# Layer 0's input norm scaled on VectorE alone, and silu's product moved ahead in its place

## The chip, the cores and the metric

The kernel runs on one core of a Trainium2 chip. The core has five engines with a queue each: TensorE (PE in the profile, its weight loads PEld), VectorE (DVE), ScalarE (ACT), GpSimd (POOL) and SyncE (SP), which here issues the DMAs. Each engine takes its instructions strictly in the order in which they were queued; engines wait for one another by semaphores. The metric is the time on the device in microseconds (us), the median of several runs; less is better.

## The reference

One inference step of two layers, a gated DeltaNet layer (layer 0) and an RWKV-7 layer (layer 1), over 1024 prompt tokens with 16 learned tokens ahead of them, and over 8 samples of 8 tokens: 1104 rows of width 1024. Both parts of the change lie in layer 0, whose start is

```python
def rmsnorm(x, w):
    xf = x.astype(jnp.float32)
    return xf * lax.rsqrt(jnp.mean(xf * xf, -1, keepdims=True) + RMS_EPS) * w.astype(jnp.float32)
...
def causal_conv(u, buf, w):
    ...
    for j in range(1, CONV_W):
        y = y + up[:, j:j + T] * w[:, j]
    return jax.nn.silu(y), up[:, up.shape[1] - (CONV_W - 1):]
...
    proj = xn @ w_in
    ...
    qkv, new_buf = causal_conv(qkv, conv_buf, conv_w)
```

The normed input `xn` is multiplied by the input projection; q, k and v go through a convolution over four tokens and silu; then come L2 norms of q and k, the chunked delta rule per head with a triangular solve, a gated norm and the output projection. There are 8 q/k heads and 16 value heads.

## The kernel before, in words

**The front.** The 1104 rows are cut into 9 blocks, numbered 0 to 8, of 128 rows (block 8 has 80). For each block `input_load` issues the DMA, `input_squares` takes the sum of squares of each row on ACT, `input_rates` makes the rate of each row (the mean on DVE, a power on POOL at line 160, and three small DVE operations at lines 162 to 164, one step of Newton's method), `input_scale` multiplies the block by the rate and by the norm's weight `nwb`, and `input_turn` transposes it on PE into PSUM (eight transposes), copies it as the high half into SBUF on ACT (line 361) and takes the low half as a difference on DVE (line 365). High and low halves serve a product in three passes, which stands in for full float32.

There are two ways of scaling in the kernel before. Blocks 0, 1, 2, 5 and 7 are scaled by one DVE instruction, which multiplies by rate and weight together (line 347). Blocks 3, 4, 6 and 8 are given to `input_rates` as `far`: the weight is multiplied on POOL (line 333), ahead of the rate, and `input_scale` then multiplies by the rate on ACT (line 345, recorded as line 115, the helper `act`). The blocks run in the order 1, 2 and 0 together, 3 and 4 together, 5, 6 and 7 together, 8.

**Places.** What each engine does when in layer 0 is written out by hand with a `Gaps` object. The projection's matmuls are the line along which time is counted: after every six matmuls of `dense_gaps` comes a place (a call of `gap`), and everything put into that place is then queued, in the order of its priority number, smaller first, and for equal numbers in the order in which it was put there. A tile of the projection (128 columns of weights by one of three token segments of 384, 384 and 336) is 24 matmuls and so four places. Blocks 3 to 8 of the front are scaled, turned and copied within the first eleven places, beside the products of the gates (`dg`) and of the first k head (`dk`). Until the first rows are there, PE multiplies identities (`busy`).

The prediction names these others of the front: the weight splits (`cast`, priority 2.9, with a copy on ACT at line 139 and a difference `wlo` on POOL at line 143), the gate operations of `gates_part` (DVE, lines 426 and 427, priority 0.5), and `vectors`, which transposes the norm vectors into PSUM and copies them out on DVE (`pcol`, line 230), and whose PSUM buffer `m` block 7 uses next.

**Convolution and silu.** `conv_plan` puts, for a segment that ends at place e: the first tap on ACT at e + 1 (priority 1.5), two taps on DVE at e + 2 and one at e + 3 (line 634), a tanh on ACT at e + 4, and silu's product on DVE at e + 5 (`silu`, lines 641 to 648: one or two products, and for the last segment a small memset). It runs for every head's q, k and v. The same places hold work of other kinds, which the prediction names by tile: `E` (line 766, `scaled`, priority 2, score scaling in `prep_plan`, which reads a PSUM bank `usc` that the next segment's `usc` matmuls fill), `zg` (line 906, `gate_out`, priority 1.7, put there only when the gate's tile is done, and which frees that tile's PSUM bank), `fss` (PE transposes of q in `query_norms`), `f<-vt` (PE transposes of v in `values_done`) and the inverse's steps (lines 690 and 692, 2.4). Segments end at e = 3, 7 or 11 after a multiple of 12 places, so silu's place e + 5 is always a multiple of four. The layer goes through eight pairs of value heads, one per q/k head, numbered 0 to 7.

The parts between the layers stand outside `manual_schedule`; their order is made by the framework's planner from simulated times (`schedule_with_timeline_sim=True`).

Of the kernel before, what the change touches and what calls it, by code (L numbers as in the profile page):

```python
# [54 lines left out]
class Stream:  # L55
# [5 lines left out]
    def fetch(self):  # L61
        if self.fetched < len(self.srcs):
            w = self.raw[self.fetched] = self.b.t(self.b.wp, [128, 4, 128], "wraw", 2)
            v = self.srcs[self.fetched]
            m = v.shape[2]
            self.b.nc.sync.dma_start(w.rearrange("p a b -> p (a b)").rearrange("p (k m) -> p k m", m=m), v)
            self.fetched += 1

    def cast(self):
        if self.made < len(self.srcs):  # L70
            hi, lo = (self.b.t(self.b.wp, [128, 4, 128], n, self.b.WB, F32R) for n in ("whi", "wlo"))
            self.b.split(self.raw.pop(self.made), hi, lo)
            m = self.srcs[self.made].shape[2]
            self.w[self.made] = [x.rearrange("p a b -> p (a b)").rearrange("p (k m) -> p k m", m=m) for x in (hi, lo)]
            self.made += 1
# [13 lines left out]
class Builder:  # L89
# [395 lines left out]
    def start(self, L, xh, xl, kh, kl, fetch, cast):  # L485

        nc = self.nc
        self.input_load(1)
        self.input_weight()
        self.input_load(2, 0, 3)  # L490
        self.gates_load()
        self.input_load(4)
        fetch(0)
        fetch(1)
        self.input_load(5)
        self.act(self.gin.nea, self.cvals[:, 0:1], AF.Square)
        for x in (self.gin.hi, self.gin.lo):
            nc.gpsimd.memset(x.bitcast(F32), 0.0)
        w = Ctx()
        w.r, w.t = {}, {}  # L500
        self.gates_clear()
        self.vectors_open()
        self.busy("m", 1, 16)

        def squares(*qs):
            w.r[qs] = self.input_rates(list(qs), self.input_squares(*qs), [q for q in qs if q in (3, 4, 6, 8)])
        rates = lambda *qs: next(w.r[qs], None)

        def begin(q, tag):
            w.t[q] = self.input_turn(q, tag, xh, xl)  # L510
            next(w.t[q])
        finish = lambda q: next(w.t[q], None)
        squares(1)
        squares(2, 0)
        rates(1)
        rates(1)
        self.input_scale(1)
        begin(1, "r")
        self.busy("f", 2, 10)
        rates(2, 0)  # L520
        rates(2, 0)
        self.input_scale(0)
        begin(0, "m")
        self.busy("f", 2, 3)
        self.input_scale(2)
        finish(1)
        begin(2, "r")
        self.busy("f", 2, 8)
        squares(3, 4)
        finish(0)  # L530
        rates(3, 4)
        w.gate = self.gates_weights()
        finish(2)
        squares(5)
        rates(3, 4)
        self.input_scale(3)
        rates(5)
        cast(0)
        cast(1)
        L.put(14, self.gates_mask, 2.9)  # L540
        self.input_load(6, 7)
        self.vectors_load()
        self.input_load(8)

        def put(g, f, *a, prio=1.0):
            L.put(g, lambda: f(*a), prio)
        for u in range(6):
            q, g, tag = 3 + u, 2 * u, "mr"[u % 2]
            if u:
                put(g - 2, self.input_scale, q, prio=0.6)  # L550
            put(g, begin, q, tag, prio=0.7)
            put(g, finish, q, prio=1.15)
        put(0, rates, 5, prio=1.2)
        put(1, squares, 6, 7, prio=1.3)
        put(2, rates, 6, 7, prio=1.25)
        put(3, rates, 6, 7, prio=1.25)
        put(5, squares, 8, prio=1.3)
        put(5, rates, 8, prio=1.35)
        put(6, rates, 8, prio=1.25)

        def gate(s, p):
            part = self.gates_part(s, p)
            next(part)
            L.put(L.now + 1, lambda: next(part, None), 0.5)
        gates = lambda s: self.dense_gaps(w.gate, kh, kl, s, "g", lambda p: gate(s, p), 64)
        return gates
# [19 lines left out]
    def conv_plan(self, ends, ft, dst, done=None):  # L586

        nc, i, t, L, fp = self.nc, self.i, self.t, self.line, self.fp
        c = Ctx()
        f = slice(128 * ft, 128 * ft + 128)  # L590
        cw = [self.cw[:, k, ft:ft + 1] for k in range(4)]
        raws, ys = [], []
        wd = lambda s: SEGS[s][1] + (24 if s == 0 else 0)
        prev = lambda s: raws[s][:, wd(s):wd(s) + 3]
        v11 = lambda x: x[:, 0:88].rearrange("p (b r) -> p b r", r=11)
        v8 = lambda x: x.rearrange("p (b r) -> p b r", r=8)
        v3 = lambda x: x.rearrange("p (b r) -> p b r", r=3)

        def load():
            c.hist = t(fp, [24, 128], "hist", 2)  # L600
            nc.sync.dma_start(c.hist, i["state_gdn_conv"][0].rearrange("b r c -> (b r) c")[:, f])

        def head():
            x = t(fp, [128, 411], "raw", 3)
            raws.append(x)
            hp = self.ps("f", 2, "hist")
            self.transpose(hp[:, 0:24], c.hist)
            nc.vector.tensor_copy(v11(x)[:, :, 0:3], v3(hp[:, 0:24]))
            nc.gpsimd.memset(x[:, 88:91], 0.0)

        def out(s, p):
            n = SEGS[s][1]
            if s == 0:
                x = raws[0]
                nc.scalar.copy(v11(x)[:, :, 3:11], v8(p[:, 0:64]))
                nc.scalar.copy(x[:, 91:411], p[:, 64:384])
            else:
                x = t(fp, [128, 411], "raw", 3)
                raws.append(x)
                nc.gpsimd.tensor_copy(x[:, 0:3], prev(s - 1))  # L620
                nc.scalar.copy(x[:, 3:3 + n], p[:, 0:n])

        def first(s):
            ys.append(t(fp, [128, 408], "cvy", 2))
            self.act(ys[s][:, 0:wd(s)], raws[s][:, 0:wd(s)], AF.Identity, scale=cw[0])
            if s == 0:
                c.last = t(fp, [128, 27], "last", 2)
                nc.gpsimd.tensor_copy(v3(c.last[:, 0:24]), v11(raws[0])[:, :, 8:11])
            elif s == 2:
                nc.gpsimd.tensor_copy(c.last[:, 24:27], prev(2))  # L630

        def tap(s, *ks):
            for k in ks:
                nc.vector.scalar_tensor_tensor(ys[s][:, 0:wd(s)], raws[s][:, k:k + wd(s)], cw[k], ys[s][:, 0:wd(s)], op0=ALU.mult, op1=ALU.add)  # L634

        def tanh(s):
            self.act(raws[s][:, 0:wd(s)], ys[s][:, 0:wd(s)], AF.Tanh, scale=0.5)

        def silu(s):
            e, y, d, n = raws[s], ys[s], dst(s), SEGS[s][1]  # L640
            one = lambda d, e, y: nc.vector.scalar_tensor_tensor(d, e, 1.0, y, op0=ALU.add, op1=ALU.mult)
            if s == 0:
                one(v8(d[:, 0:64]), v11(e)[:, :, 0:8], v11(y)[:, :, 0:8])
                one(d[:, 64:384], e[:, 88:408], y[:, 88:408])
            else:
                one(d[:, 0:n], e[:, 0:n], y[:, 0:n])
                if n < 384:
                    nc.vector.memset(d[:, n:384], 0.0)

        def ending():  # L650
            lp = self.ps("f", 2, "last")
            self.transpose(lp[0:27, 0:128], c.last)
            c.ls = t(fp, [27, 128], "lasts", 1)
            nc.vector.tensor_copy(c.ls, lp[0:27, 0:128])

        def store():
            nc.sync.dma_start(self.o["s_gdn_conv"][0].rearrange("b r c -> (b r) c")[:, f], c.ls[0:24])
            nc.sync.dma_start(self.o["p_gdn_conv"][0, 0][:, f], c.ls[24:27])

        L.put(ends[0] - 11, load, 2)  # L660
        L.put(ends[0] - 2, head, 2)
        for s, e in enumerate(ends):
            L.put(e + 1, lambda s=s: first(s), 1.5)
            L.put(e + 2, lambda s=s: tap(s, 1, 2), 2)
            L.put(e + 3, lambda s=s: tap(s, 3), 2)
            L.put(e + 4, lambda s=s: tanh(s), 2)
            L.put(e + 5, lambda s=s: silu(s), 2)
            if done is not None:
                L.put(e + 8, lambda s=s: done(s), 2.2)
        L.put(ends[2] + 5, ending, 2.5)  # L670
        L.put(ends[2] + 8, store, 3)
        return out
# [1959 lines left out]
```

## Time and profile before

| | us |
|---|---|
| median of 3 runs | 2236.03 (2235.1 to 2237.79) |
| the profiled execution's own time | 2233.16 |
| its span, first to last instruction | 2231.5 |
| PE busy | 2133.0 (96% of the span) |
| DVE busy | 1426.3 (64%) |
| ACT busy | 1266.2 (57%) |
| POOL busy | 1245.4 (56%) |

The mean granted clock of TensorE was 0.983. Busy times are of one profiled execution; they say how much an engine had to do, not whether anybody waited for it. Rows in order of time give the start and the length in us, engine, line, operation, what is written and read, the count of merged instructions, and in brackets the idle time of the engine ahead of the row and what ended it.

### The profile page before, as it was taken

Reading aid. Unit: us, or ns where it says so; the run is one execution under the profiler, and the core shown is the slowest. Engines: PE = TensorE matmul, PEld = TensorE weight load, DVE = VectorE, ACT = ScalarE, POOL = GpSimd, SP = SyncE. Lnnn points to the kernel's source line nnn. Section 1 sums busy time; section 2 is a strip of 40 time slices with the busy share of each in tenths; the row PEclk is TensorE's granted clock in tenths of the full one; section 3 lists DMA queues with packets and bytes.
Section 4 is the critical chain, followed back from the end, with each engine's and each line's share of the span. In section 5 each row is a group of like instructions: output and inputs, shape, how many; then the busy total and the mean of one; then the engine's idle time right before and its main releaser. Section 6 shows DMA issues by size and latency. Waiting matters only on the chain.

```text
span 2231.5 us, 55344 instructions
## 1 busy us (share of the span) xinstructions
PE 2133.0 (96%) x20382; PEld 1964.7 (88%) x20382; DVE 1426.3 (64%) x3634; ACT 1266.2 (57%) x3655; POOL 1245.4 (56%) x1894
## 2 busy tenths in 40 slices
PE   7889999999999999989999999999999999999997
PEld 6888989898998999878998999998988977888886
DVE  6868586766757585975435762767546347667764
ACT  6636565556655565645433464746546466667663
POOL 4518668585858585625240442237768636666663
PEclk9999999999999999999999999999999999999997
DMA  3324242424243342436244234587885566655532
GB/s 115 85 63 133 71 118 74 109 82 113 79 116 96 85 122 68 136 77 174 91 141 112 71 98 169 193 254 197 232 240 145 156 188 165 170 149 171 163 115 91
DMA packets 495400, 291.61 MB, mean 131 GB/s; under 512 B 222345, under 2 KB 480506, under 8 KB 495130
## 3 DMA queue, kind: packets, MB, share of 16 engines
q1 hardware_dynamic: 495130, 288.08, 46.1%
q8 instruction: 161, 2.64, 0.5%
q14 instruction: 109, 0.89, 0.1%
HBM read 195.66 MB, written 92.30 MB: 129 GB/s over the span
## 4 chain that ended last, share of the span: by engine, by line
PE 64%; DVE 15%; ACT 6%; POOL 5%; DMA 5%; issue 4%; SPq 1%; DVEq 0%; POOLq 0%; ACTq 0%
PE d L129 13%; PE dz L129 7%; PE dv L129 7%; PE rA L133 5%; PE rA L129 5%; PE zo L129 3%; PE do L129 3%; DVE cvy L634 3%; POOL invT L692 2%; PE fG L129 2%; PE dk L129 2%; POOL invtmp L690 2%; DVE E L766 1%; DMA wraw<-in_gdn_w_out 1%; PE dq L129 1%
## 5 line engine op out<-in xcount | busy, mean ns | idle before, releaser
L143 POOL TENSOR_TENSOR wlo<-wraw,whi 128x512 fp32r<-128x512 f32 x190 | 250.3, 1318 | 220.8 <-ACT whi L139 203.5
L692 POOL TENSOR_TENSOR invT<-invT,invtmp 72x31 f32<-72x31 f32 (+36 forms) x341 | 213.1, 625 | 26.7
L634 DVE SCALAR_TENSOR_TENSOR cvy<-raw,cw,cvy 128x408 f32<-128x408 f32 (+2 forms) x288 | 206.9, 718 | 31.2 <-ACT cvy L115 27.1
L690 POOL TENSOR_TENSOR invtmp<-invA,invT 72x31 f32<-72x31 f32 (+36 forms) x341 | 204.5, 600 | 20.4 <-POOL invT L678 0.7
L129 PE MATMUL d<-xc,whi 128*128 128x384 f32 (+1 forms) x640 | 179.2, 341 | 1.5 <-ACT whi L139 1.2
L139 ACT CAST whi<-wraw 128x512 fp32r<-128x512 f32 x238 | 145.7, 613 | 33.0 <-DMA wraw<-in_rwkv_w_rkvz 19.0
L129 PE MATMUL dv<-xc,whi 128*128 128x384 f32 (+1 forms) x480 | 154.1, 342 | 0.0
L129 PE MATMUL dz<-xc,whi 128*128 128x384 f32 (+1 forms) x480 | 152.8, 341 | 0.0
L115 ACT ACTIVATE w<-rA,nbp 128x128 f32<-128x128 f32 x144 | 45.0, 363 | 155.1 <-PE rA L129 152.7
L129 PEld LDWEIGHTS d<-xc,whi 128*128 128x128 f32 x640 | 117.3, 190 | 4.0 <-ACT whi L139 1.5
L160 POOL TENSOR_TENSOR ors<-ovar,cvals 128x6 f32<-128x6 f32 x24 | 34.1, 1420 | 134.5 <-DVE ovar L1122 134.5
L129 PE MATMUL d<-xc,wlo 128*128 128x384 f32 (+1 forms) x320 | 104.5, 336 | 2.2 <-DVE wlo L143 2.2
L129 PE MATMUL dz<-xa,whi 128*128 128x384 f32 (+1 forms) x288 | 102.8, 357 | 0.0
L129 PE MATMUL dv<-xa,whi 128*128 128x384 f32 (+1 forms) x288 | 102.1, 355 | 0.0
L129 PE MATMUL d<-xa,whi 128*128 128x384 f32 (+1 forms) x336 | 99.1, 338 | 1.7 <-POOL xa L143 1.0
L1930 POOL TENSOR_SCALAR y<-y,mv,grs 128x64 f32<-128x64 f32 x132 | 81.5, 634 | 34.5 <-DVE grs L164 29.2
L129 PEld LDWEIGHTS dv<-xc,whi 128*128 128x128 f32 x480 | 89.0, 188 | 3.5 <-issue 3.0
L129 PEld LDWEIGHTS dz<-xc,whi 128*128 128x128 f32 x480 | 90.4, 191 | 0.6 <-issue 0.2
L959 POOL TENSOR_SCALAR Sb<-Sb,eglb 128x128 f32<-128x128 f32 x128 | 82.5, 658 | 6.0 <-DMA Sb<-in_state_gdn 5.6
L129 PE MATMUL d<-xh,whi 128*128 128x384 f32 (+1 forms) x256 | 82.5, 334 | 0.2 <-ACT xh L139 0.2
L129 PE MATMUL d<-xl,whi 128*128 128x384 f32 (+1 forms) x256 | 82.6, 336 | 0.0
L129 PE MATMUL d<-xh,wlo 128*128 128x384 f32 (+1 forms) x256 | 82.4, 335 | 0.0
(546 smaller groups left out, 7236.4 us busy)
## 6 DMA issues: line engine op xcount, KB each, us to landing
wraw<-in_gdn_w_in SPq DMA_DIRECT2D x96, 256.0 KB
wraw<-in_rwkv_w_rkvz SPq DMA_DIRECT2D x74, 256.0 KB
Sb<-in_state_gdn SPq DMA_DIRECT2D x64, 256.0 KB
wraw<-in_rwkv_w_o SPq DMA_DIRECT2D x48, 256.0 KB
E<-drow SPq DMA_DIRECT2D x24, 384.0 KB
attn<-drow SPq DMA_DIRECT2D x24, 384.0 KB
wraw<-in_gdn_w_out SPq DMA_DIRECT2D x36, 256.0 KB
out_s_gdn<-Sb SPq DMA_DIRECT2D x32, 256.0 KB
```

The costliest lines, as they stand in the source:

```text
L115: return self.nc.scalar.activation(out, in_, func, bias=bias, scale=scale, **kw)
L129: self.nc.tensor.matmul(out, lhsT, rhs, start=start, stop=stop)
L133: self.nc.tensor.matmul(out, lhsT, rhs, start=start, stop=True, skip_group_check=True)
L139: nc.scalar.copy(hi, x)
L143: e.tensor_tensor(lo, x, hi.bitcast(F32), op=ALU.subtract)
L160: self.nc.gpsimd.tensor_tensor(y, x, half.broadcast_to(sh), op=ALU.pow)
L634: nc.vector.scalar_tensor_tensor(ys[s][:, 0:wd(s)], raws[s][:, k:k + wd(s)], cw[k], ys[s][:, 0:wd(s)], op0=ALU.mult, op1=ALU.add)
L690: v.tensor_tensor(tmp, A[:, j, j + 1:32].unsqueeze(2).broadcast_to([nb, n, m]), Tv[:, j, 0:m].unsqueeze(1).broadcast_to([nb, n, m]), op=AL ...
L692: v.tensor_tensor(Tv[:, j + 1:32, 0:m], Tv[:, j + 1:32, 0:m], tmp, op=ALU.subtract)
L766: nc.vector.scalar_tensor_tensor(E[:, tt, h], p_[s][:, 128 * tt:128 * tt + 128], c.bp[:, 3 * s + tt, h:h + 1], E[:, tt, h], op0=ALU.mult, ...
L959: nc.gpsimd.tensor_scalar(Sb[g][:, u], Sb[g][:, u], self.eglb[:, hv, 4 * g + u:4 * g + u + 1], None, op0=ALU.mult)
L1930: nc.gpsimd.tensor_scalar(y[:, q], y[:, q], mv[:, q, 0:1], P.rs[:, q:q + 1], op0=ALU.subtract, op1=ALU.mult)
```

## The change

It has two parts. In `start`, `squares` no longer hands `input_rates` a list of `far` blocks, so no block is multiplied on POOL or scaled on ACT: all nine go through the one DVE instruction of `input_scale`. It stands where the ACT product stood, at priority 0.6 of its place for blocks 4 to 8 and directly ahead of the first place for block 3. In `conv_plan`, silu's product has priority 1.7 instead of 2.

```diff
         def squares(*qs):
-            w.r[qs] = self.input_rates(list(qs), self.input_squares(*qs), [q for q in qs if q in (3, 4, 6, 8)])
+            w.r[qs] = self.input_rates(list(qs), self.input_squares(*qs))
         rates = lambda *qs: next(w.r[qs], None)
...
             L.put(e + 4, lambda s=s: tanh(s), 2)
-            L.put(e + 5, lambda s=s: silu(s), 2)
+            L.put(e + 5, lambda s=s: silu(s), 1.7)
             if done is not None:
```

## The prediction

> **What bounds the kernel now.** I read stretches of the span first, then the chain of waits, then the rows in order of time where that chain leaves TensorE (PE).
>
> ```profile
> 15.00:25.00 10.00, 7.51 (x47) 6.42 (x48) 8.35 (x19) 6.17 (x13) 6.87 (x4) 0.83 0.46 157
> 35.00:45.00 10.00, 7.22 (x30) 5.95 (x31) 7.13 (x12) 5.28 (x10) 5.27 (x7) 0.71 0.00 1
> 125.00:135.00 10.00, 7.14 (x55) 6.45 (x56) 9.65 (x25) 2.12 (x5) 1.28 (x1) 0.99 0.10 26
> 250.00:300.00 50.00, 50.00 (x530) 47.31 (x529) 26.63 (x72) 27.53 (x87) 26.22 (x48) 1.00 0.43 118
> ```
>
> A stretch's row gives its length, then the busy time of PE, weight loads, VectorE (DVE), ScalarE (ACT) and GpSimd (POOL), then the granted clock. From 250 on PE is never idle: work saved there on another engine is worth nothing unless PE waits for it by name. In the front (15 to 45) and in the first head pair (to 135) PE idles a quarter of the time, and from 35 to 45 its clock was 0.71. Every queue is in order and every wait relative, so a microsecond won in the front reaches the end, if nothing later eats it.
>
> ```profile
> 28.89 2.35 DVE rs L164
> 37.61 1.15 ACT x L115
> 41.43 2.98 DVE x L347
> 132.90 0.42 DVE vt L641
> 133.98 12.59 PE dz L129 x66
> ```
>
> The chain (start, length, what) runs through the very products that change: a 128x1 operation that took 2.35, block 6's product on ACT, block 7's on DVE. At 133 it passes from DVE (silu's product `vt`) to PE for good.
>
> **First edit: the four products.** All forms of the input block's scaling, min/median/max in ns:
>
> ```profile
> L347 DVE SCALAR_TENSOR_TENSOR x<-x,rs,nwb x5: 1283/1285/3380, 7.0 to 41.4; 128x1024 f32<-128x1024 f32 x5
> L333 POOL TENSOR_TENSOR x<-x,nwb x4: 2358/2708/3351, 14.3 to 41.0; 128x1024 f32<-128x1024 f32 x3, 80x1024 f32<-80x1024 f32 x1
> ```
>
> Blocks 3, 4, 6 and 8 lose 2.36 to 3.35 on POOL each and an ACT product (1.15 at 23.51 and 37.61), and gain 1.28 on DVE: 4 x 1.28 = 5.1 more for DVE. The rows in order of time show what POOL's products cost DVE, and when PE gets each block:
>
> ```profile
> 13.80 4.58 DVE L347 SCALAR_TENSOR_TENSOR x<-x,rs,nwb 128x1024 f32<-128x1024 f32 x2
> 14.27 6.34 POOL L333 TENSOR_TENSOR x<-x,nwb 128x1024 f32<-128x1024 f32 x2 [1.09 <-ACT junk L115]
> 16.80 1.49 PE L129 MATMUL fbusy<-ident 128*128 128x128 f32 x6
> 19.73 0.59 ACT L361 CAST xa<-r 128x512 fp32r<-128x512 f32 x1 [1.48 <-PE r L126]
> 21.60 0.69 DVE L365 TENSOR_TENSOR xc<-r,xa 128x512 fp32r<-128x512 f32 x1
> 23.51 1.15 ACT L115 ACTIVATE x<-x,rs 128x1024 f32<-128x1024 f32 x1 [1.30 <-DVE ss L334]
> 24.72 0.66 PE L126 MATMUL m<-ident,x 128*128 128x128 f32 x4 [1.46 <-ACT x L115]
> 25.25 2.54 POOL L143 TENSOR_TENSOR wlo<-wraw,whi 128x512 fp32r<-128x512 f32 x2 [1.13 <-ACT whi L139]
> 27.73 1.04 PE L126 MATMUL r<-ident,x 128*128 128x128 f32 x8
> 28.82 2.39 POOL L333 TENSOR_TENSOR x<-x,nwb 128x1024 f32<-128x1024 f32 x1 [1.03 <-ACT junk L115]
> 31.26 1.28 DVE L347 SCALAR_TENSOR_TENSOR x<-x,rs,nwb 128x1024 f32<-128x1024 f32 x1
> 32.69 0.63 PE L126 MATMUL m<-ident,x 128*128 128x128 f32 x4 [1.83 <-DVE x L347]
> 35.23 1.22 DVE L426 TENSOR_SCALAR rows<-rows 16x384 f32<-16x384 f32 x1
> 36.48 0.55 DVE L427 SCALAR_TENSOR_TENSOR ay<-ax 16x384 f32<-16x384 f32 x1
> 38.81 1.62 PE L126 MATMUL r<-ident,x 128*128 128x128 f32 x8 [2.57 <-ACT x L115]
> 40.97 2.36 POOL L333 TENSOR_TENSOR x<-x,nwb 80x1024 f32<-80x1024 f32 x1 [4.73 <-ACT junk L115]
> 43.30 1.53 POOL L160 TENSOR_TENSOR rs<-ss,cvals 128x1 f32<-128x1 f32 x1
> 46.40 0.66 PE L126 MATMUL m<-ident,x 128*128 128x128 f32 x4 [0.74 <-DVE pcol L230]
> 49.41 0.72 PE L126 MATMUL r<-ident,x 80*128 80x80 f32 x8
> ```
>
> Three times a POOL product stands beside a DVE operation that ends late: the pair at 13.80 takes 4.58 for 2.57 (2.0 lost), the 128x1 operation 2.35 until POOL ends at 31.21 (2.2), block 7's product 2.98 for 1.28 (1.7). That is 5.9 that comes back for the 5.1 added, so DVE's sum hardly changes; what changes is when PE gets its blocks.
>
> Block 3: DVE is through block 2 at 13.80 + 2.57 = 16.4, not 18.4. PE's filler ends at 18.3, so block 2's transposes start there and not 0.7 later, behind a DVE difference; ACT's copy behind them moves from 19.73 to 19.0, ending 19.6, and DVE, no longer late, takes the difference at 19.6 instead of 21.60. From there to the product is 23.51 - 21.60 = 1.9, then 1.28: block 3 is ready at 22.8 instead of 24.66. PE starts it at 22.85, lead 1.9.
>
> Blocks 4 and 5: block 4's product follows on DVE to 24.3 (a 0.2 sum operation stands between), ahead of PE's need, which is 27.73 less the lead, 25.9. Block 5's rate needs a POOL power, which waits while DVE holds a product (43.30: 1.53, ending 0.4 after that product) to 24.7; then POOL's two weight splits, 2.54, hold DVE's rate operations to 27.3. They end at 27.8, block 5 at 29.1. PE, which took 32.69 - 1.83 - 24.72 = 6.14 between the two blocks, arrives at 29.0. Lead 3.6.
>
> Block 6: from block 5's end (32.54) DVE has the differences, rates and two gate operations to 37.03, 4.5 of work; after 29.1 that ends at 33.6, and the product at 34.9 instead of ACT's 38.76. Lead 3.9; PE still waits about 2.3.
>
> Blocks 7 and 8: then DVE does differences, sum, product 7 unheld, differences, rates and the `pcol` copy, by about 40.5. PE needs 46.40 - 0.74 - 38.81 = 6.85 after block 6: 41.75, lead 4.65, if its clock stays down as in the 0.71 stretch; with a clock that recovers it is held by `pcol` at 40.5, lead 5.9. Block 8 follows on DVE behind `pcol` and four small copies, ready at about 42.5; PE wants it 49.41 - 46.40 = 3.0 after block 7, at 44.7 or 43.5. Its load waits for block 3's buffer, so it goes out earlier too, and ACT's squares only gain room. I take 5.0 for the front, nearer to the slow clock, since PE still waits 2.3 where it waited 2.57.
>
> Bounds: at worst the two products on PE's path that are new (3 and 6) each take the longest DVE row, 3.38, and 4.2 of the 5.0 go. At best all four waits in PE's brackets (6.6) and the slow clock between 35 and 45 (10.00 x 0.29 = 2.9) go, 9.5. What hides block 4's and block 8's products is PE's own queue (1.6, and 1.0 to 2.2, to spare); without that cover each would cost up to its 1.28.
>
> The Trainium skill, page "SBUF — State Buffer", section "Who interferes with whom", says that a VectorE instruction with two SBUF inputs and a GpSimd instruction that reads SBUF block each other for a whole instruction. The 28.82 and 28.89 rows agree (both end at 31.2). It speaks against the change too: the new products read two SBUF tensors, and the weight splits are still on POOL. By it alone the splits' 2.54 may fall on a product in full, which is the first rival below.
>
> The clock: after the wait of 2.57 at 38.81 eight transposes took 1.62, after that of 1.83 at 32.69 the rows were quick (four in 0.63). The Trainium skill, page "TensorE: Matmul & The Clock Gate", section "What's actually happening", has the clock set by activity in windows of about 3.4 us that run freely. By that rule a wait of 2.3 can fall either way, which would be a front of 4.65 or of 5.9; the trace agrees in so far as waits of 1.83 and 2.57 fell differently.
>
> **Second edit: silu at 1.7 instead of 2.** Silu's place is always a multiple of four, and of DVE's work there it passes only two kinds: the third score scaling (`E`, two operations at priority 2) and a gate product `zg` at 1.7, which was queued later.
>
> ```profile
> 82.84 0.94 PE L129 MATMUL usc<-K 128*128 128x128 f32 x6 [1.49 <-DVE E L766]
> 132.36 0.54 DVE L906 SCALAR_TENSOR_TENSOR zg<-zg,dz 128x384 f32<-128x384 f32 x1
> 132.82 0.50 DVE L641 SCALAR_TENSOR_TENSOR vt<-raw,cvy 128x336 f32<-128x336 f32 x1
> 133.46 0.52 PE L126 MATMUL f<-ident,vt 128*128 128x128 f32 x3 [2.14 <-DVE vt L648]
> 198.14 0.55 PE L126 MATMUL fss<-ident,Q 128*128 128x128 f32 x3 [0.36 <-DVE Q L641]
> 310.45 1.23 DVE L641 SCALAR_TENSOR_TENSOR K<-raw,cvy 128x336 f32<-128x336 f32 x1
> 311.74 0.94 PE L129 MATMUL usc<-K 128*128 128x128 f32 x6 [1.33 <-DVE K L648]
> 317.54 1.64 DVE L766 SCALAR_TENSOR_TENSOR E<-usc,bp,E 128x128 f32<-128x128 f32 x6
> 319.82 0.55 PE L126 MATMUL fss<-ident,Q 128*128 128x128 f32 x3 [0.52 <-ACT raw L621]
> 925.84 0.55 PE L126 MATMUL fss<-ident,Q 128*128 128x128 f32 x3 [0.50 <-ACT raw L621]
> ```
>
> At 132.36 `zg` stood ahead of `vt`, for which PE waits: 0.46 earlier, of which PE keeps 0.3, as its next matmul needs the bank that `zg` frees. Seven `fss` (pairs 1 to 7; first and last shown) wait 0.36 to 0.57 for Q, which stands behind six `E` of 1.64; the last two, 0.55, now come after it. All seven waits go: about 3.5. Nobody waits for these two `E` soon: their bank's next user is ten places on. K's five waits of 1.3 (the first at 311.74) stay: `usc` needs K and also the bank that `E` frees, and both together end when they did; only 0 to 0.55 each, so 0 to 2.8, if K's product, 1.23 because it is held, slips past POOL. I take 0. In the first pair Q goes ahead of the `E` that `usc` waits for at 82.84, two times up to 0.6 more; PE's 2.14 wait at 133.46 covers it, and without that cover it costs 1.2.
>
> Sum: 5.0 + 0.3 + 3.5 = 8.8. The profiled execution took 2233.16 (span 2231.5 and 1.66 around it), which makes 2224.4. The median of the three runs is 2236.03, 2.9 above it, and I predict that median's counterpart: 2227.2.
>
> **The rivals.** *Held products.* POOL's two splits (2.54) fall on a new product and not on the small rate operations, and the lead loses 2.5: 2229.7. For it: both are at 23 to 27. Against: PE has 1.6 of slack at block 4. *No gain from the order.* If Q's product is itself held, as K's at 310.45 is (1.23 for about 0.5), the 3.5 stays: 2230.7; with both, 2233.2.
>
> *Slower: DVE becomes the front's bound.* It is at 8.35 of 10 from 15 to 25. If the holds return through the splits and the gate operation (2.54, and 0.7 at 35.23, whose 1.22 stands beside a neighbour's 0.55), and the silu order adds its uncovered 1.2: 5.1 - 5.9 + 3.2 + 1.2 = 3.6 later, 2239.6. It decides from the point where the holds exceed 0.8. Against it: from 35 to 45, holds included, DVE was busy 7.13 of 10. The Trainium skill's page "Perfetto Trace Analysis", section "Optimizing Scalar/DVE Operations", advises moving work to ScalarE where VectorE is saturated, the reverse of this edit; the trace does not show it saturated in that stretch.
>
> *The planner.* Between the layers the order is made by a planner's simulated times, which may fall differently. No row prices that; between 250 and 300 PE has no idle time to lose, and I put 5, the size of the front's change, either way around the forecast.
>
> **How the numbers follow.** Forecast 0.55 (its own range 2225 to 2229); held products 0.15; order without gain 0.12; both 0.07; slower 0.05; planner 0.06. About 0.2% (4.5) is what can be told from no change. Faster by more: 0.55 + 0.12 + 0.06 + 0.03 = 0.76; slower by more: 0.02 + 0.01 = 0.03; the rest 0.21. The range goes up to both of the first two rivals together, 2233.2, and down half-way to the front's best (2.2) with K's whole 2.8: 2222.2.
>
> **What would show it.** Right: no product row on POOL; nine on DVE, eight of them at 1.28; PE starts block 5 near 29, block 7 near 41.5; `vt` ahead of `zg` and PE's handover near 128; no `fss` wait in pairs 1 to 7, K's waits at 1.3. Wrong: DVE product rows of 2 to 3 beside `wlo`, `fss` waits unchanged, or PE waits after 1050 that were not there.

## The result, and the profile after

Seven executions of the changed kernel have a median of 2220.93 (2218.54 to 2229.42), beside 2235.10 of the kernel before in the same measurement: a ratio of 0.9948, 95% interval 0.9930 to 0.9965. A second measurement (e1 below) gave 0.9933 (0.9911 to 0.9955). It is faster, by 0.5 to 0.7%. The forecast was 2227.2. The median 2220.93 lies 1.3 below the lower end of the forecast's range; the ratio times the median on which the forecast stands, 0.9948 x 2236.03 = 2224.4, lies inside it. The profiled execution took 2229.18, with a span of 2227.4; it is one of the two longest of the seven, and a fall of the clock in its profile (below) is at least part of the reason.

The stretches of the profile after, with the columns as before:

```profile
15.00:25.00 10.00, 9.47 (x62) 8.62 (x61) 9.61 (x24) 7.23 (x17) 3.41 (x3) 0.83 0.49 150
35.00:45.00 10.00, 9.96 (x58) 8.52 (x58) 9.19 (x25) 4.90 (x13) 1.87 (x3) 0.83 0.01 2
125.00:135.00 10.00, 7.79 (x47) 7.13 (x46) 9.52 (x27) 2.57 (x6) 1.42 (x1) 1.00 0.22 67
250.00:300.00 50.00, 50.00 (x529) 47.27 (x528) 25.75 (x68) 27.77 (x87) 26.13 (x48) 1.00 0.45 118
```

In the front TensorE is busy 9.47 and 9.96 of 10 where it was busy 7.51 and 7.22. GpSimd falls from 6.87 to 3.41 and from 5.27 to 1.87; VectorE rises, to 9.61 at most. The granted clock from 35 to 45 is 0.83 where it was 0.71. All forms of the scaling, and then the front in order of time:

```profile
L347 DVE SCALAR_TENSOR_TENSOR x<-x,rs,nwb x9: 1268/1284/1286, 7.0 to 38.9; 128x1024 f32<-128x1024 f32 x8, 80x1024 f32<-80x1024 f32 x1
```

```profile
22.40 0.63 PE L126 MATMUL m<-ident,x 128*128 128x128 f32 x4 [0.53 <-DVE ss L334]
25.25 1.20 DVE L163 SCALAR_TENSOR_TENSOR rn_t<-rn_t,ss 128x1 f32<-128x1 f32 x1
25.38 1.04 PE L126 MATMUL r<-ident,x 128*128 128x128 f32 x8
28.35 0.60 PE L126 MATMUL m<-ident,x 128*128 128x128 f32 x4
33.87 1.06 PE L126 MATMUL r<-ident,x 128*128 128x128 f32 x8 [2.00 <-DVE x L347]
39.41 0.60 PE L126 MATMUL m<-ident,x 128*128 128x128 f32 x4
42.37 0.72 PE L126 MATMUL r<-ident,x 80*128 80x80 f32 x8
```

The nine products take 1.27 to 1.29 each: none is held. PE starts blocks 3 to 8 at 22.40, 25.38, 28.35, 33.87, 39.41 and 42.37; before it was 24.72, 27.73, 32.69, 38.81, 46.40 and 49.41. The leads are 2.3, 2.4, 4.3, 4.9, 7.0 and 7.0. One wait is left, 2.00 for block 6. The clock falls behind it, as it fell behind the 2.57 before, but for about half as long: stretches of 1 us show it at 0.50 from 35.7 to 39.1, and before from 39.2 to 46.0.

The first head pair and pair 1 in the same view:

```profile
69.26 2.38 DVE L641 SCALAR_TENSOR_TENSOR K<-raw,cvy 128x336 f32<-128x336 f32 x1 [0.61 <-ACT raw L115]
70.42 0.85 POOL L721 TENSOR_SCALAR_AFFINE_SELECT E<-E 128x768 f32<-128x768 f32 x1
78.88 0.94 PE L129 MATMUL usc<-K 128*128 128x128 f32 x6 [2.97 <-DVE E L766]
129.24 0.52 PE L126 MATMUL f<-ident,vt 128*128 128x128 f32 x3 [1.71 <-DVE vt L648]
145.41 0.22 PE L129 MATMUL uU<-TT,invA 32*32 32x32 f32 x2 [0.23 <-DMA TT<-g_u]
149.68 0.22 PE L129 MATMUL fU<-TT,invA 32*32 32x32 f32 x2 [1.28 <-DMA TT<-g_u]
310.71 0.50 DVE L641 SCALAR_TENSOR_TENSOR K<-raw,cvy 128x336 f32<-128x336 f32 x1
311.80 0.94 PE L129 MATMUL usc<-K 128*128 128x128 f32 x6 [0.61 <-DVE E L766]
319.21 0.49 PE L126 MATMUL fss<-ident,Q 128*128 128x128 f32 x3
```

Three things are new. K's last product of pair 1 takes 0.50 and not 1.23, and the wait at `usc` is 0.61 and not 1.33; the prediction had left it where it was. The wait for Q at `fss` is gone, as predicted. And in pair 0's merges PE waits for transfers of the inverse (`TT<-g_u`), 0.23 and 1.28, where it did not wait in the profile before. After the second of these waits the granted clock falls:

```profile
150.00:155.00 5.00, 5.00 (x56) 4.63 (x47) 0.91 (x2) 1.75 (x5) 0.00 (x0) 0.67 0.54 150
155.00:160.00 5.00, 5.00 (x53) 4.03 (x54) 0.71 (x2) 0.82 (x2) 0.00 (x0) 0.50 0.02 3
160.00:165.00 5.00, 5.00 (x65) 4.33 (x62) 2.35 (x7) 0.64 (x2) 0.00 (x0) 0.80 0.00 0
```

In the profile before the clock was 1.00 in all three. How far PE is ahead of the kernel before can be read from any instruction that both have: its start before, less its start after. For `fss` of pair 1 that is 319.82 - 319.21 = 0.6. Followed in this way through one profiled execution of each kernel, by the start that the instruction has in the profile before:

| start before | after | e1 | e2 | e3 | e4 | e5 | e6 | e7 | e8 | e9 | e11 | e12 |
|---|---|---|---|---|---|---|---|---|---|---|---|---|
| 60.0, the front is done | 7.0 | 5.8 | 6.9 | 0.4 | 5.2 | 7.1 | 0.4 | -1.7 | 7.3 | -1.7 | 0.4 | 7.1 |
| 86.1, behind pair 0's squares | 2.4 | 3.7 | 4.5 | -2.8 | 2.5 | 5.1 | -1.1 | -3.4 | 6.5 | -2.5 | -1.0 | 7.0 |
| 134.1, behind the handover | 4.1 | 5.1 | 4.5 | -1.3 | 2.8 | 6.0 | -1.2 | -2.9 | 6.8 | -2.7 | -1.3 | 7.0 |
| 152.0, in pair 0's merges | 4.4 | 5.3 | 5.1 | -0.9 | 3.1 | 6.6 | -0.6 | -2.2 | 7.5 | -2.3 | -0.3 | 6.9 |
| 166.1, behind them | -1.4 | -4.8 | 4.1 | -1.8 | 1.7 | 6.0 | -1.6 | -9.5 | 6.8 | -3.0 | -0.9 | 6.2 |
| 320.1, pair 1 | 0.7 | -2.8 | 3.9 | 0.2 | 3.8 | 8.1 | 0.5 | -8.9 | 8.8 | -1.9 | -0.9 | 8.2 |
| 926.0, pair 7 begins | 5.3 | 1.2 | 0.6 | 6.8 | 8.9 | 12.8 | 5.6 | -9.0 | 12.7 | 0.3 | -1.0 | 13.8 |

Kernels with the same front differ by up to 2.1 at 60.0 (e3, e6 and e11 beside e7 and e9), and e11, which changes nothing behind pair 0, gained 8.0 between 1163 and 2209. So one profile prices a stretch only where the instructions show a reason; for whole kernels the medians count. In e5, e8, e11 and e12 the merges themselves stand a place later, so the row 152.0 does not compare them with the others. Four rows of the table have a reason that the traces show.

*60.0.* What sets kernels with the same front apart is the clock. From 30 to 50 its mean is 0.91 after and in e2, e5, e8 and e12, with leads of 6.9 to 7.3, and 0.83 in e1 and e4, with 5.8 and 5.2. With the old front it is 0.83 before and in e3, e6 and e11 (0.0 to 0.4), and 0.76 and 0.75 in e7 and e9 (-1.7). At the same 0.83 the new front is 4.8 to 5.8 ahead; the rest of the 7.0 is the clock of this execution.

*86.1.* K's last product of pair 0 takes 2.38 after, but 1.42 in e1, which is the same kernel, and 2.38 in e11, which has neither edit. So neither edit is shown to cause this hold; it differs from one execution to the next. Q's new place costs about 0.5 there: at `usc` PE waits 2.97 after and 2.44 in e4 beside the long product, 2.02 in e5 and 1.57 in e8 beside one of 1.41.

*152.0 to 166.1.* The waits for the transfers are not the lead's doing. e6 and e7 have the front of before and no lead, and wait as well:

```profile
154.25 0.22 PE L129 MATMUL fU<-TT,invA 32*32 32x32 f32 x2 [0.81 <-DMA TT<-g_u]
156.29 0.26 PE L129 MATMUL fU<-TT,invA 32*32 32x32 f32 x2 [1.23 <-DMA TT<-g_u]
```

So do e3 (0.62) and e9 (0.48). And the transfers move with the lead: the first read of the inverse is issued 12.5 behind the handover before (146.00 less 133.46), 13.0 after (142.20 less 129.24), and 12.6 to 13.1 in the other kernels with the early merges. What sets the profile before apart is its clock between the handover and the merges, first before, then after:

```profile
135.00:140.00 5.00, 5.00 (x24) 5.00 (x24) 4.66 (x15) 0.45 (x1) 0.99 (x2) 0.68 0.43 137
135.00:140.00 5.00, 5.00 (x31) 5.00 (x30) 1.86 (x6) 3.39 (x8) 1.55 (x4) 1.00 0.22 62
```

Counted from the handover (134.1), PE reached the merges (148) 0.8 to 1.2 later there than in the other kernels with the early merges. That goes most of the way to explain why it did not wait.

*320.1 to 926.0.* With the first edit alone (e2) 3.3 of the lead go in this stretch. 2.4 of them go between 784 and 800, mostly at a sixth product of K that is held (1.22, and PE waits 1.31 for it), which in the profile before took 0.80 and was not waited for.

The stretch from 166 to 926 of before, and the same instructions after:

```profile
166.00:926.00 760.00, 746.81 (x6358) 696.07 (x6357) 534.10 (x1417) 453.02 (x1466) 537.98 (x883) 1.00 0.36 99
```

```profile
167.50:920.70 753.20, 746.00 (x6358) 696.55 (x6357) 520.63 (x1417) 454.15 (x1465) 539.13 (x881) 1.00 0.37 100
```

6.8 shorter. PE's idle time falls from 13.2 to 7.2; VectorE does the same 1417 operations in 13.5 less. The waits of PE by what ended them (sum, times, longest), before:

```profile
PE usc L129 <- DVE K L648: 6.6, 5, 1.3
PE fss L126 <- ACT raw L621: 2.5, 5, 0.5
PE fss L126 <- DVE Q L641: 0.9, 2, 0.6
```

and after:

```profile
PE usc L129 <- DVE E L766: 3.7, 6, 0.6
PE msc L129 <- DVE Sb L968: 1.0, 6, 0.2
```

### The profile page after: what moved, and what is told of

Same layout as the page of the kernel before. It is cut to its first block, busy times and chain, and to the rows that moved or that the text cites. A ratio compares the mean times of both kernels' runs of the same rounds, so it can differ in the third digit from the quotient of the medians.

```text
span 2227.4 us, 55333 instructions
## 1 busy us (share of the span) xinstructions
PE 2142.1 (96%) x20382; PEld 1977.4 (89%) x20382; DVE 1411.3 (63%) x3638; ACT 1265.0 (57%) x3651; POOL 1237.8 (56%) x1890
## 4 chain that ended last, share of the span: by engine, by line
PE 68%; DVE 13%; POOL 6%; DMA 5%; ACT 4%; issue 3%; SPq 1%; DVEq 0%; POOLq 0%; ACTq 0%
PE d L129 14%; PE dz L129 7%; PE dv L129 7%; PE rA L133 6%; PE rA L129 5%; PE zo L129 3%; PE do L129 3%; PE dk L129 3%; DVE cvy L634 2%; POOL invT L692 2%; PE fG L129 2%; POOL invtmp L690 2%; PE dq L129 2%; DMA wraw<-in_gdn_w_out 1%; DVE invT L692 1%
## 5 line engine op out<-in xcount | busy, mean ns | idle before, releaser
L959 POOL TENSOR_SCALAR Sb<-Sb,eglb 128x128 f32<-128x128 f32 x128 | 88.8, 706 | 5.9 <-DVE usc L752 2.2
```

The source lines that it names most:

```text
L959: nc.gpsimd.tensor_scalar(Sb[g][:, u], Sb[g][:, u], self.eglb[:, hv, 4 * g + u:4 * g + u + 1], None, op0=ALU.mult)
```

## The experiments

The theory after this reading: the front's lead is real and larger than forecast, but part of it is lost in pair 0, at the squares and at the merges; and the second edit is worth more than forecast, by K's waits. The rival: the pieces do not add up in this way, one edit carries the whole, and the rest is scatter. What shortens K's product became a question of its own from e6 on. Each measurement stands beside the kernel before on the same chip.

**e1 to e4: the change again, and its parts.** e2 has only the first edit, e3 only the second, e4 both with Q's silu of pair 0 back at 2.

e1: 

> The change once more, beside its halves. Theory: about 11 us under the kernel before (9 to 14), with a spread of several us between executions, because the head pair 0 merge now meets its DMAs: where an execution is quick, PE shows no lowered clock between 145 and 165.

e2: 

> Only the input norm on VectorE; silu at 2 as before. Theory (both halves count): PE is 7.0 ahead at block 7 as with both edits, about 5 ahead at the handover of pair 0, and the time falls by 4 to 6 us. Rival (the front's lead is eaten on the way to pair 0's merge, whose DMAs then hold PE): falls by 0 to 2 us. Seven waits of PE for Q's product in pairs 1 to 7 stay at 0.4 to 0.6, and the waits for K's at 1.3.

e3: 

> Only silu's priority at 1.7; the front as before. Theory (both halves count): the waits for Q go, those for K fall from 1.3 to 0.6, pair 0 loses up to 2.5 at its score matmuls and wins 0.3 to 1 at the handover; the time falls by 4 to 6 us. Rival (the second edit carries all): falls by 9 to 12 us.

e4: 

> Both edits, but q's silu of head pair 0 stays at 2, behind its E. Theory (in pair 0 Q ahead of E costs for good what PE waits longer there, 3.0 against 1.5): 1 to 2.5 us faster than with both edits whole. Rival (later waits of PE for DVE in pair 0 cover it, as the prediction had it): the same within 1 us.

```diff
# e4, shortened; late is 1.7 unless given (e2: the first edit alone; e3: the second alone)
-            L.put(e + 5, lambda s=s: silu(s), 1.7)
+            L.put(e + 5, lambda s=s: silu(s), late)
...
-    kept(g.Q, s, "Q", 5))
+    kept(g.Q, s, "Q", 5), late=1.7 if j else 2)
```

| | median (executions) | ratio, 95% |
|---|---|---|
| e1, both | 2219.39 (6) | 0.9933 (0.9911 to 0.9955) |
| e2, the first edit | 2229.19 (6) | 0.9966 (0.9953 to 0.9980) |
| e3, the second edit | 2223.20 (6) | 0.9949 (0.9935 to 0.9964) |
| e4, both, Q of pair 0 at 2 | 2220.90 (5) | 0.9932 (0.9919 to 0.9944) |

The first edit alone gives 0.34% (7.6), the second 0.51% (11.4), both 0.67% (15.0): less than the sum, 19.0, though the intervals allow it. e4 is no different from both: in the table both lose 4.6 of the lead from 60 to 86 where e4 loses 2.7, and gain 1.7 from there to the handover where e4 gains 0.3. But e1, the same kernel as after, loses 2.1 and gains 1.4, so these two profiles do not price Q's place; that the 0.5 it costs at `usc` is given back, as the prediction said of its cover, rests on the equal ratios. Of the expectations, e1 (9 to 14), e2 and e3 (4 to 6 each) all came out above their theory, e3 at its rival's 9 to 12; that rival, the second edit carrying all, does not fit e2's 7.6.

**e5 and e11: pair 0's merges one place later.** e5 has both edits, e11 neither.

```diff
-        for s, at in enumerate((0, 1, 4)):
+        for s, at in enumerate((0, 1, 4) if j else (1, 2, 5)):
```

e5: 

> Both edits, and pair 0's three merges put one place later in the line (at 1, 2, 5 in place of 0, 1, 4), so that their DMA reads of the inverse have landed. Theory A (the front's lead is thrown away where pair 0's merges meet their transfers): in the profile of both edits TensorE waits 0.23 and 1.28 us for TT at 145.41 and 149.68, and the granted clock then falls to 0.50 to 0.67 in two executions of both edits and costs 4.8 to 9.7 us. With the merges a place later these two waits are gone, the clock stays at 1.00 from 140 to 170, and the time falls: 1.5 us for the waits in every execution, and the executions near 2229 go, so 2215 to 2219 against 2219.4 to 2220.9 of both edits. Rival B (the waits only move: what reads the merged inverse is late instead): TensorE waits 1 to 2 us more at its first use of the merged inverse, after 160, and the time is 2219 to 2222. Rival C (the fall of the clock has nothing to do with these waits): the clock falls in 140 to 170 all the same.

e11: 

> The kernel before with nothing but pair 0's merges one place later. In the profile before TensorE does not wait for TT at the merges, so theory A (the merges only limit a kernel whose front has a lead of 4 to 7 us) gives no difference: 2233 to 2237, a ratio within 0.2% of 1. Rival B (the later merges are better in themselves, by the clock or by fewer waits after 160): 2229 to 2232.

e5 measured 2219.17 (6 executions, 2215.63 to 2221.83), ratio 0.9922 (0.9901 to 0.9943); e11 2235.05 (12), ratio 0.9996 (0.9982 to 1.0011). In e5's order of time the only wait left between 140 and 165, and its stretch at 155:

```profile
158.43 0.91 PE L129 MATMUL uU<-TT,invA 64*64 64x64 f32 x12 [0.77 <-DVE invA L865]
```

```profile
155.00:160.00 5.00, 4.24 (x40) 3.54 (x39) 3.23 (x7) 1.17 (x3) 1.27 (x1) 1.00 0.41 110
```

The two waits for the transfers are gone, the clock stays at 1.00, and the lead of 6.0 at the handover is 6.0 at 166. That is what theory A forecast for the profile; some of it becomes the 0.77, as rival B had it. In the median the gain (0.9922 beside 0.9933) is within the intervals. What can be seen is the upper end: three of thirteen executions of both edits took 2229 to 2233, and none of the eighteen with later merges (e5, e8, e12) over 2222; e10, which has them too, goes up to 2224.55. Two of those three were profiled, and both show the fall of the clock; for the third it is inferred. That the later place prevents the fall is not shown: six of the nine profiles with the early merges are without it too, and the one of e7, which has it, took 2234.08, no more than e7's median. On the kernel before the later merges are worth nothing (e11), and no time shows that they are worth more beside the new front.

**e6 and e7: K's order alone, Q's order alone**, both on the kernel before.

```diff
# e6, shortened; late is 2 unless given; e7 has late=1.7 for Q in place of K
-            L.put(e + 5, lambda s=s: silu(s), 2)
+            L.put(e + 5, lambda s=s: silu(s), late)
...
-    kept(g.K, s, "K", 6))
+    kept(g.K, s, "K", 6), late=1.7)
```

e6: 

> The kernel before, with only K's silu product at 1.7 (Q's and V's at 2, GpSimd's four products kept). In the kernel before K's last product takes 1.21 to 1.24 us in five pairs, beside three GpSimd products on Sb, against 0.48 where it runs alone, and TensorE then waits 1.3 for it. Theory A (the order frees K's product from that hold): the product takes 0.50, the wait becomes 0.6 for the two E that now follow it, and pairs 1 to 6 gain 0.7 each, about 4 us: 2230 to 2232; the waits for Q stay at 0.5 to 0.6. Rival B (the hold goes only because Q's gain shifts the pair against GpSimd): K's product still takes 1.2, TensorE waits 1.3 + 0.5 for the E behind it, so 1.8, and the kernel is slower by 3 us. What the prediction said (K's waits stay, at 1.3): no difference.

e7: 

> The kernel before, with only Q's silu product at 1.7 (K's and V's at 2, GpSimd's four products kept). Theory A (each of K and Q has its own gain): the seven waits of 0.5 to 0.6 for Q are gone, K's of 1.3 stay, so 3.5 us less over pairs 1 to 7, and 0.5 to 1.2 more at pair 0's second squares, of which the later handover gives some back: 2231 to 2233. Rival B (one gain sets the other off: the shift of the pair against GpSimd frees K's product too): K's product takes 0.5 here as well and the waits fall to 0.6 or less: 2226 to 2228.

e6 measured 2225.98 (8), ratio 0.9957 (0.9937 to 0.9977); e7 2234.95 (12), ratio 1.0005 (0.9989 to 1.0020). Pair 1 of e6 in order of time, where VectorE's tap (line 634) of the same place stands behind the product:

```profile
310.92 0.50 DVE L641 SCALAR_TENSOR_TENSOR K<-raw,cvy 128x336 f32<-128x336 f32 x1
312.01 0.94 PE L129 MATMUL usc<-K 128*128 128x128 f32 x6 [0.61 <-DVE E L766]
312.58 1.30 DVE L634 SCALAR_TENSOR_TENSOR cvy<-raw,cw,cvy 128x408 f32<-128x408 f32 x2
319.41 0.49 PE L126 MATMUL fss<-ident,Q 128*128 128x128 f32 x3
```

and of e7:

```profile
319.93 1.22 DVE L641 SCALAR_TENSOR_TENSOR K<-raw,cvy 128x336 f32<-128x336 f32 x1
321.20 0.94 PE L129 MATMUL usc<-K 128*128 128x128 f32 x6 [1.31 <-DVE K L648]
328.70 0.55 PE L126 MATMUL fss<-ident,Q 128*128 128x128 f32 x3
333.56 0.24 PE L126 MATMUL fhist<-ident,hist 24*128 24x24 f32 x1 [0.52 <-ACT fss L115]
```

K's order by itself takes away K's hold and the waits for Q too, though Q still stands behind all six `E`: 7.2 from 166 to 926, as much as both. Theory A had the waits for Q stay; they go because VectorE comes to Q earlier. Q's order by itself takes the wait at `fss` away and sets it up again five microseconds on: the transpose `fhist` needs the buffer that ACT's squares of Q free, and ACT does them in its own order. All waits of e7 of that kind:

```profile
PE fhist L126 <- ACT fss L115: 3.6, 7, 0.5
```

Seven, 3.6 together, for the seven of 3.4 that went. Theory A failed for Q; rival B, that the shift would free K as well, failed too. From 166 to 926 e7 gains 0.5.

**e9: the hold itself.** The order of before, and only the four multiplications that stand beside K's last product on ScalarE.

```diff
# shortened at ...
-                nc.gpsimd.tensor_scalar(Sb[g][:, u], Sb[g][:, u], ..., None, op0=ALU.mult)
+                self.act(Sb[g][:, u], Sb[g][:, u], AF.Identity, scale=...) if h == 1 and g == 0 and j < 7 else nc.gpsimd.tensor_scalar(...)
```

> The kernel before, its silu at 2 and GpSimd's four products kept; only the four multiplications on Sb (128x128 each) that GpSimd runs beside K's last product of pairs 1 to 7 (309.63 to 312.15 in the profile before) are given to ScalarE, which is idle there. Theory A (the first cost of the old order is a hold: K's product, queued behind two E, meets GpSimd's run of multiplications): K's product falls from 1.22 to 1.24 to about 0.5 with the order unchanged, TensorE's wait for K from 1.3 to about 0.6, and with VectorE ahead by 0.7 the waits of 0.5 to 0.6 for Q go as well: 1.2 to 1.3 a pair over six pairs, 7 to 8 us, 2227 to 2229. Rival B (the order is what counts: K's product must stand ahead of the E): the wait for K stays at 1.3 and the waits for Q at 0.5: no difference, 2233 to 2236. Rival C (GpSimd's next long operation, the weight's second split of 1.29, moves up into the product): the product stays at 1 to 1.3, no difference.

Measured: 2229.12 (12), ratio 0.9976 (0.9962 to 0.9990). First GpSimd and the tap in the profile before, then e9:

```profile
309.63 2.52 POOL L959 TENSOR_SCALAR Sb<-Sb,eglb 128x128 f32<-128x128 f32 x4
312.13 1.29 POOL L143 TENSOR_TENSOR wlo<-wraw,whi 128x512 fp32r<-128x512 f32 x1
312.34 2.20 DVE L634 SCALAR_TENSOR_TENSOR cvy<-raw,cw,cvy 128x408 f32<-128x408 f32 x2
```

```profile
313.31 0.49 DVE L641 SCALAR_TENSOR_TENSOR K<-raw,cvy 128x336 f32<-128x336 f32 x1
313.86 0.94 PE L129 MATMUL usc<-K 128*128 128x128 f32 x6 [0.60 <-DVE K L648]
314.07 1.28 POOL L143 TENSOR_TENSOR wlo<-wraw,whi 128x512 fp32r<-128x512 f32 x1 [1.50 <-DVE lasts L654]
314.46 2.02 DVE L634 SCALAR_TENSOR_TENSOR cvy<-raw,cw,cvy 128x408 f32<-128x408 f32 x2
321.71 0.55 PE L126 MATMUL fss<-ident,Q 128*128 128x128 f32 x3 [0.28 <-DVE Q L641]
```

Without the multiplications the product takes 0.49 in the old order, and the wait is 0.60. So the long product was a hold by GpSimd, and rival B (the order is what counts for K) falls. What is left shows a second hold: the two taps take 2.20 before, beside the weight split, 2.02 in e9, where the split still lies on them, and 1.30 in e6. With it e9 keeps seven waits for Q, of 0.23 to 0.32, where theory A had them gone, and it gains 3.3 between 166 and 926 where e6 gains 7.2. From before to after the two holds, 0.71 to 0.75 on six of K's last products (0.30 on a seventh) and 0.88 to 0.90 on the taps of all seven pairs, make 10.9 of the 13.5 by which VectorE's time fell.

In the new order it is GpSimd that is held: after, the same four multiplications take

```profile
310.39 3.00 POOL L959 TENSOR_SCALAR Sb<-Sb,eglb 128x128 f32<-128x128 f32 x4
```

and not 2.52. The Trainium skill, page "SBUF — State Buffer", section "Who interferes with whom", says that the order of issue decides which of the two engines is blocked. These rows agree, in that the same operations hold VectorE in one order and GpSimd in the other. Why a product that starts 0.24 into a multiplication is held through the next (before) and one that starts 0.32 into one is hardly held (after), no run here settles.

**e8, e10, e12: better versions.** e8 is e5 with Q's silu of pair 0 at 2. e10 is e8 with the first head's two additions on Sb one place later, behind K's product and the `E`. e12 is the first edit, K's order alone and the later merges.

e8: 

> Both edits, pair 0's merges one place later, and Q's product of pair 0 back at 2. Theory A (the merges are what throws the lead away, Q's product of pair 0 costs nothing that the handover does not give back): no waits for TT at the merges, clock 1.00 from 140 to 170, and within 1.5 us of the kernel with the merges alone: 2215 to 2219. If Q's product of pair 0 does cost: 1 to 2 us below it. If the merges are no cost (Rival B): 2219 to 2222, like both edits with Q back.

e10: 

> Both edits, pair 0's merges one place later, Q's product of pair 0 at 2, and the two additions on Sb of each pair's first head (0.68 each on VectorE, with their matmuls) one place later, so that they stand behind K's last product and the two E and no longer ahead of them. Theory A (what is left of K's wait, 0.61 in six pairs, is VectorE's queue in that place): the six waits go, 3.7 us: 2213 to 2215. Rival B (the additions then stand ahead of the next place's work, the X and the tap, and TensorE waits there): 2217 to 2220, with new waits of 0.5 to 1 for X or usc.

e12: 

> The first edit, the second for K's silu alone (Q's and V's products stay at 2), and pair 0's merges one place later. Theory A (of the second edit only K's order carries anything; Q's by itself moved its wait of 0.5 to the next transpose): the front's lead of about 7 is kept past 166, K's last product takes 0.50, TensorE waits 0.6 for the E and not for Q, and the time is that of the kernels with Q's and V's order too, 2217.3 to 2219.2, so 2215 to 2220. Rival B (with K's order in place Q's is worth its seven waits of 0.5): the waits for Q come back at 0.3 to 0.5 and the time is 2220 to 2223.

| | median (executions) | ratio, 95% |
|---|---|---|
| e8 | 2217.32 (6) | 0.9912 (0.9893 to 0.9932) |
| e10 | 2222.31 (6) | 0.9946 (0.9926 to 0.9967) |
| e12 | 2218.14 (6) | 0.9935 (0.9918 to 0.9951) |

e8 has the lowest median of all and is 0.2% below both edits by the ratios, within the intervals. e12 does without Q's and V's order and has the median of the others; its ratio is against a before of 2231.76 in that measurement. e10 missed its 2213 to 2215:

```profile
419.93 2.39 POOL L955 TENSOR_SCALAR wexp<-w,bmask 64x128 f32<-64x128 f32 x4 [4.56 <-PE fsw L129]
420.37 1.47 DVE L641 SCALAR_TENSOR_TENSOR K<-raw,cvy 128x336 f32<-128x336 f32 x1
423.22 0.94 PE L129 MATMUL msc<-Q,K 128*128 128x128 f32 x6 [1.12 <-DVE Sb L968]
```

K's wait went, but GpSimd's next run now starts with K's product, which is held again, 1.47, and PE waits 1.12 for the additions instead. The waits at `fhist` are there too, seven of 0.43 to 0.52.

## Why the prediction was right, and where not

**The front: right in its mechanism; of the 2.0 by which it was too small most is the clock.** Forecast leads of 1.9, 3.6, 3.9 and 4.65 or 5.9 at blocks 3, 5, 6 and 7 stand beside 2.3, 4.3, 4.9 and 7.0; the new product for block 6 still made PE wait (2.3 forecast, 2.00 measured), and the split fell on a rate operation and not on a product, but only one of the two: 1.20 at 25.25 and not 2.54. The forecast took the slow clock; in this execution it was low for half as long, PE took 5.54 from block 6 to block 7 where 6.85 were forecast, and `pcol`, forecast at 40.5, was through at 38.7. Where the clock was as low as before (e1 and e4) the lead is 5.8 and 5.2, beside 5.0. The rival "held products" is out: all nine take 1.27 to 1.29. The slower rival has its point in 15 to 25, where VectorE rose to 9.61 of 10, but the holds of 3.2 that it needs did not come. The hold of 1.0 at 25.25 is more than the 0.8 from which the rival was to decide, and PE led all the same; the gate operation's 1.17 (at 30.66) is no new hold, as it took 1.22 before.

**That the lead reaches the end: wrong in part.** The step that failed is "a microsecond won in the front reaches the end, if nothing later eats it", read from the waits of one profile before. What ate into it in the runs: in pair 0 PE waits 2.97 at `usc` where it waited 1.49, by Q's new place (0.5) and by a product of K that GpSimd holds for 2.38 in some executions; at the merges it waits 1.5 for transfers, as kernels without a lead do, and in some executions the clock falls there, which with these waits takes 6 to 10; and in e2 3.3 go by pair 7. How much of the lead arrives, only the times say: by e2 the first edit as a whole is worth 7.6 (4.5 to 10.5). In the profiles of e5, e8 and e12 the leads of 6.0 to 7.0 at the handover are still 6.0 to 6.8 behind the merges.

**The handover: right.** `vt` comes ahead of `zg`, PE's transposes start at 129.24 (forecast near 128), and the lead grows by 0.43 there, of which PE keeps 0.3 at its next product, as forecast.

**The seven waits for Q: right in number, wrong in cause.** They went, 3.4 for 3.5. But not because Q stands ahead of two `E`: e7 makes that move alone and the waits go over to `fhist`, 3.6. They go because VectorE has been freed earlier in the pair (e6).

**K's waits: the step that failed.** "only 0 to 0.55 each, so 0 to 2.8, if K's product, 1.23 because it is held, slips past POOL. I take 0." The product is held no longer: 0.50 for 1.23 and waits of 0.61 for 1.33. The row was in the prediction, 1.23 and called held; it was priced by the wait that it ends, and not by what it does to everything behind it on VectorE. With the taps VectorE gains 1.1 a pair from the start of K's product to the next reading of the squares (310.45 to 315.32 before, 310.71 to 314.46 after), and that carries Q's waits. From 166 to 926 PE gained 6.7 after, 8.6 in e3 and 7.2 in e6, beside a forecast of 3.5 for the second edit there, and in e2 it lost 3.5; the time of e3, 0.51% or 11.4 (8.0 to 14.5), says the same.

**The planner**: behind 1050 the engines' operations stand in the same order in both profiles. **The rivals** "no gain from the order" and "both" are out by e3.

The front gained by the mechanism that was forecast, the second edit by another; that the range held is in part luck. Both parts came out larger than their terms, the first edit at 7.6 (e2) for 5.0 and the second at 11.4 (e3) for 3.8, and both together at less than their sum. By the first measurement's ratio the forecast time is inside the range, by e1's, 0.9933 x 2236.03 = 2221.0, it would be below the 2222.2.

What stays open is the rest of the difference between e3's time (11.4) and what its pairs show (8.6); the scatter behind 1163, 8.0 in e11, is larger than that.

## What to carry to other kernels

An operation that a trace shows at two or three times its usual length is a cost for everything queued behind it on its engine, and not only for the wait that it ends: ask what a change does to that hold before pricing the order. A wait that one engine's order takes away can come back at the next buffer that another engine frees, so follow the buffer and not the matmul. And a wait that shows up together with a lead need not come from it: before naming the cause, look for the wait in a kernel without the lead, and at the clock in the stretch ahead of it.

## What the runs showed of the hardware

In pair 0's merges the granted clock fell to 0.50 after a wait of PE of 1.28 (after), 1.16 (e1) and 1.23 (e7), among 32x32 products, and by the stretches of 5 us stayed down for about 10, 20 and 14; it did not fall there after 1.22 in e4, nor after 0.48 to 0.81 in e2, e3, e6 and e9. In the front the same wait for block 6, 2.00 to 2.05 in all eight profiles with the first edit, left the clock from 30 to 50 at 0.83 in two, at 0.91 in five and at 1.00 in one (e10). The Trainium skill, page "TensorE: Matmul & The Clock Gate", section "What's actually happening", has windows of activity that run freely, by which the same wait can fall either way; that fits e4 beside e7 and the eight fronts, but no view here shows the windows. A hold between VectorE and GpSimd was worth 0.7 to 0.9 for operations whose own length is 0.5 to 0.65 (K's product, the taps), and a start 0.5 earlier beside the same four multiplications (0.82 into them before, 0.32 after) moved it from VectorE to GpSimd.
